# Weights of the last projection in the slab pool, three deep, and a last output tile in three pieces

## The chip, the cores and the metric

The kernel runs on one core of one Trainium2 chip. The metric is the device time of one execution in microseconds, as the median of several runs. A profile is one further execution, recorded by the hardware profiler; its times count from the start of its span. PE is TensorE's matmul unit, PEld its weight loads, DVE is VectorE, ACT is ScalarE, POOL is GpSimd and SP is SyncE, which here issues all DMAs.

## The reference

One step of a two-layer decoder trunk, for 1024 prompt tokens and 8 sample tokens that share the weights (1032 tokens, 1024 features). The first layer joins dilated attention and a state-space scan; the second, where the change lies, is an mLSTM with 8 heads of 256:

```python
def odd_layer(hn, w_in, w_out, ...):
    u = hn @ w_in                                  # 1024 -> q, k, v, o, i, f, z
    ...                                            # convolution, gates
    h, c, n, m = mlstm_chunked(q, k, v, i_t, logf, c0, n0, m0)
    h = sigmoid(o_pre) * h
    h = head_norm(h, norm_w).reshape(b, L, 2048)
    out = (h * silu(z)) @ w_out                    # 2048 -> 1024: the last projection
    return out, ...

hp = hp + mp;  hs = hs + ms                        # residual
y = rmsnorm(h, final_norm_w)                       # over 1024 features, then scaled
```

The sample tokens also update a memory of 8 x 8 x 256 x 256 numbers (`mcs`), which is read and written whole.

## The kernel before, in words

**Arithmetic.** Features lie on partitions, tokens along the free axis. Each float32 operand is split into a high part (ScalarE, line 90: `A.copy(hi, src)`) and a low part (VectorE, line 91: source minus high part), both of type float32r, and a product is three matmuls: high x high, low x high, high x low.

**The last projection** (from line 1588). The weight matrix comes in 32 pieces of 128x1024 (I number them #0 to #31), two for each of eight output rows of 128 features, and this twice: first for tokens 0 to 511 (`hv` 0), then for the other 520 (`hv` 1). `out_f` (line 918) makes one output row: 16 steps over the 2048 inputs, three matmuls in each for each piece of tokens. With `hv` 0 there is one piece of 512, with `hv` 1 there are two, of 264 and 256. Where `done` is not given, the pieces alternate within each step, and each is evicted at the end (VectorE adds the residual, line 935). For the last row alone (`f == 7` of `hv` 1), `done` is given: the pieces run one after the other, and after each comes its part of the closing norm, whose steps are slipped into the next piece's matmuls after its steps 7 and 11 (first the sums over partitions, `stat`, line 188, then the broadcast of the result, line 207), or follow behind the last piece. Then eight scalings (line 221) make the output, with a store for every two.

**Weights.** The class `Weights` loads a piece into a raw buffer (`rawp`, three buffers), and `fetch` splits it into `wh` and `wl`: into two slabs if `slabs` is above zero, which it then counts down, and otherwise into the pool of the input projection's weights, which holds two pairs. `next(ahead)` fetches until more than `ahead` pieces are ready and hands out the first. `wstream` calls it once in eight steps. Two pieces are fetched ahead of the loop (lines 1614 and 1616).

**Buffers.** `S(...)` takes a slab: one of 15 buffers of 128x1040 that the convolutions, the gate, the value weights (`wvh`, `wvl`), the blocks of the sample memory (`dC`), the output rows (`y2`), part of the second half's operands and the final output share. A pool hands out its buffers in the program's order: an instruction that first writes a slab goes after all slabs that were asked for before it in the program, and waits until one is free. The raw pool holds the weights as loaded and, for `hv` 0, also the eight loads `hld` of the projection's operand, each of which is split into `oh` and `ol` (`hT_half`).

**Beside it.** The sample memory's last group runs during `hv` 0: `step(j)` (line 1407) loads block j+1, scales block j on ScalarE, runs eight operations on it on VectorE and stores it; `pump` puts one step after the third row, three after the fourth, three after the fifth and the rest after the sixth.

**Order.** Nothing here sets the order on an engine by hand: the framework's planner runs through the whole program with its own costs, sends each instruction to its engine's queue when its operands and its buffer are there, the earlier in the program first, and so writes one fixed order for each engine and for SP's DMA queue. On the chip each queue then runs strictly in that order.

Of the kernel before, what the change touches and what calls it, by code (L numbers as in the profile page):

```python
# [28 lines left out]
def body(ctx, tc, I, O):  # L29
# [26 lines left out]
    def S(name, dt=F32):  # L56
        return slab.tile([128, 1040], dt, tag="S", name=name)
# [13 lines left out]
    def MM(name="mm"):  # L71
        return ps.tile([128, 512], F32, tag="mm", name=name, bufs=PS_MM)

    def X(name="ax"):
        return ps.tile([128, 512], F32, tag="ax", name=name, bufs=8 - PS_MM)

    def TMP(name="tmp"):
        return tmpp.tile([128, 520], F32, tag="tmp", name=name)

    def D(name, shape):  # L80
        return dr.tile(shape, F32, name=name)
# [33 lines left out]
    class Weights:  # L115
# [8 lines left out]
        def load(self, ahead=1):  # L124
            while len(self.raws) < min(ahead, len(self.srcs)):
                self.raws.append(raw_load(*self.srcs[len(self.raws)]))
# [83 lines left out]
    def hsum(acc, src, first, dve=False):  # L210
        q = acc if first else TMP("sq")[:, : src.shape[-1]]
        if dve:
            V.tensor_tensor(q, src, src, mult)
        else:
            A.activation(q, src, AF.Square)
        if not first:
            V.tensor_tensor(acc, acc, q, add)
# [11 lines left out]
    def pairs(tiles):  # L229
        return lambda k, c0, w: tiles[k // 2][:, (k % 2) * 520 + c0 : (k % 2) * 520 + c0 + w]  # L230
# [88 lines left out]
    def bpump(n):  # L319
        for _ in range(n):  # L320
            if bg:
                bg.popleft()()
# [68 lines left out]
    def pump(n=1):  # L391
        for _ in range(n):
            if side:
                side.popleft()()
# [304 lines left out]
    for f in range(12):  # L699
        w = wq0.next()  # L700
        raw = conv_raw()
        o = S("cout")
# [164 lines left out]
    h1d = D("h1d", [8, 128, T])  # L867
# [47 lines left out]
            r, hi, lo = (t.rearrange("p (j t) -> p j t", j=2)[:, :, :n] for t in (src(p), aop[hv][0][p], aop[hv][1][p]))  # L915
            split(hi, lo, r)

    def out_f(wq, nk, ops, hv, res, dst, done=None):
        n = 520 if hv else 512
        r = TMP("res")  # L920
        load(r[:, :n], res)
        if dst is None:
            dst = r
        pieces = ((0, 264, MM("po")), (264, 256, X("po"))) if hv else ((0, 512, MM("po")),)
        def mms(i, wt, piece):
            c0, m, p = piece
            w, o = wt
            ah, al = (ops[hv][u](i, c0, m) for u in range(2))
            ws = slice(o, o + 128)
            for q, (wt, at) in enumerate(((w[0], ah), (w[0], al), (w[1], ah))):  # L930
                PE.matmul(p[:, :m], wt[:, ws], at, start=i == 0 and q == 0, stop=i == nk - 1 and q == 2)  # L931

        def evac(piece):
            c0, m, p = piece
            V.tensor_tensor(dst[:, c0 : c0 + m], p[:, :m], r[:, c0 : c0 + m], add)

        if done is None:
            for i in range(nk):
                wt = wq(i)
                for piece in pieces:  # L940
                    mms(i, wt, piece)
            for piece in pieces:
                evac(piece)
        else:
            wts = [wq(i) for i in range(nk)]
            steps = deque()
            for piece in pieces:
                for i in range(nk):
                    mms(i, wts[i], piece)
                    if steps and i in ((7, 11) if nk == 16 else (4, 10)):  # L950
                        steps.popleft()()
                evac(piece)
                new = done(dst, piece[0], piece[1])
                steps.extendleft(new[1::-1])
                steps.extend(new[2:])
            while steps:
                steps.popleft()()
        return dst[:, :n]

    def wstream(wts):  # L960
        st_ = {"n": 0}

        def get(i):
            if st_["n"] % 8 == 0:
                st_["w"] = wts.next()
            o = (st_["n"] % 8) * 128
            st_["n"] += 1
            return st_["w"], o

        return get  # L970
# [23 lines left out]
    for f in range(12):  # L994
        w = wq0.next()
# [10 lines left out]
        for c in range(3):  # L1006
            t = TMP("gz")
            c0 = c * CH
            if f >= 8:
                a = TMP("al")  # L1010
                n = min(CH, NP - c0)
# [16 lines left out]
            if c < 2:  # L1028
                o = (f % 2) * 520 + c0
                n = min(CH, 512 - c0)  # L1030
                V.scalar_tensor_tensor(gA[-1][:, o : o + n], t[:, :n], 0.5, a[:, :n], mult, mult)
            if c > 0:
                n = max(512 - c0, 0)
# [6 lines left out]
    def operand(hv, u):  # L1040
        def f(i, c0, w):
            if i < 8:
                return pairs(yop[hv][u])(i, c0, w)
            return pairs(aop[hv][u])(i - 8, c0, w)

        return f
# [47 lines left out]
    ops = [[operand(hv, u) for u in range(2)] for hv in range(2)]  # L1094
    wst = wstream(wqo)
    for hv in range(2):
        n = 520 if hv else 512
        c0 = 512 * hv
        if hv:
            h1 = [S("h1") for _ in range(4)]  # L1100
        for f in range(8):
            dst = pairs(h1)(f, 0, n) if hv else None
# [3 lines left out]
            dst = out_f(wst, 12, ops, hv, I["xT"][:, f, c0 : c0 + n], dst, xn1_tail if hv and f == 7 else None)  # L1106
# [408 lines left out]
    for h in range(8):  # L1515
# [3 lines left out]
        for j in range(4):  # L1519
            t_ = 4 * h + j  # L1520
            if h == 0 and j < 2:
                if j == 0:
                    wts = [wq1.next(1), wq1.next(0)]
# [8 lines left out]
            else:  # L1532
                w = wq1.next()
# [6 lines left out]
            o = S("cout")  # L1540
# [11 lines left out]
        for j in range(2):  # L1552
            w = wq1.next()
# [31 lines left out]
        if h2 == 1:  # L1585
            tail.append(lambda g=g: dml_group(g))

    wqf = Weights([(I["wo1"][f][:, o * 1024 : o * 1024 + 1024], 1024) for _ in range(2) for f in range(8) for o in range(2)])

    hld = deque()  # L1590

    def hT_load(hv, ks):
        for k in ks:
            r = S("hld") if hv else rawp.tile([128, 1040], F32, tag="raw", name="hld")
            rv = r.rearrange("p (j t) -> p j t", j=2)
            load(rv[:, :, :512], hTd[2 * k : 2 * k + 2, :, 512 * hv : 512 * hv + 512].rearrange("j p t -> p j t"))
            hld.append(rv)

    def hT_half(hv, mh, ml, ks):
        n = 520 if hv else 512  # L1600
        for k in ks:
            al = S if hv and k < KB else XS
            mh.append(al("oh", F32R))
            ml.append(al("ol", F32R))
            if not hld:
                hT_load(hv, (k,))
            rv = hld.popleft()
            hi, lo = (t.rearrange("p (j t) -> p j t", j=2) for t in (mh[k], ml[k]))
            if hv:
                G.tensor_scalar(rv[:, :, 512:520], hss[:, 2 * k : 2 * k + 2], 1.0, None, mult)  # L1610
            split(hi[:, :, :n], lo[:, :, :n], rv[:, :, :n])
# [36 lines left out]
    ops = [[pairs(m) for m in mixA], [pairs(m) for m in mixB]]  # L1648
    wst = wstream(wqf)
    for hv in range(2):  # L1650
        n = 520 if hv else 512
        c0 = 512 * hv
        y2 = box[hv] = []
        for f in range(8):
            if f % 2 == 0:
                y2.append(S("y2"))
            dst = pairs(y2)(f, 0, n)
            if hv and f == 7:
                bpump(40)
                out_f(wst, 16, ops, hv, h1d[f][:, c0 : c0 + n], dst, last)  # L1660
                continue
            out_f(wst, 16, ops, hv, h1d[f][:, c0 : c0 + n], dst)
            hsum(yacc[:, hv * 520 : hv * 520 + n], dst, f == 0)
            if hv == 0 and f == 0:
                while tail:
                    tail.popleft()()
                store(O["mn"], nout)
            if hv == 0 and f in (1, 2):
                while dprep and f == 2 or len(dprep) > 2:
                    dprep.popleft()()  # L1670
            if hv == 0:
                pump((0, 0, 1, 3, 3, 2, 0, 0)[f])
            bpump(2)
            if hv == 0 and f == 5:
                hT_load(1, range(3))
            if hv == 0 and f == 6:
                store(O["mms"], dm4)
                store(O["mns"], dn4)
                pump(40)
                hT_half(1, *mixB, range(KB))  # L1680
                hT_load(1, range(3, KB + 4))
            if hv == 0 and f == 7:
                hT_half(1, *mixB, range(KB, KB + 2))
                wqf.fetch()
                hT_load(1, range(KB + 4, 8))
                hT_half(1, *mixB, range(KB + 2, 8))
                wqf.fetch()
        if hv == 0:
            bg.extend(fin_norm(0, 0, 512))
# [174 lines left out]
```

## Time and profile before

| | us |
|---|---|
| runs | 2125.18, 2133.5, 2126.53 |
| median | 2126.53 |
| the profiled execution | 2130.37 |
| its span | 2128.5 |
| TensorE's matmuls busy | 2088.0 (98%) |
| weight loads busy | 1873.7 (88%) |
| VectorE busy | 1348.8 (63%) |
| ScalarE busy | 869.3 (41%) |
| GpSimd busy | 478.0 (22%) |

The profiled execution took 1.9 us more than its span; both are one execution, 3.8 us over the median of the timed runs. Matmuls overlap in the records (one lasts longer than the distance to the next), so the pitch from start to start is what counts. A timeline row gives start, busy time, engine, line and operation, output and inputs, shapes and count, and in brackets the idle time before it with what ended it. Rows of several equal instructions that follow each other are merged (x2 and so on).

### The profile page before, as it was taken

The page shows a single profiled execution, that of the slowest core. Times are in us where ns is not written, and L with a number is a line of the kernel's source. Part 1 is how long each engine was busy: PE and PEld are TensorE (multiplying, and loading weights), DVE is VectorE, ACT ScalarE, POOL GpSimd, SP SyncE. Part 2 cuts the span into 40 slices and gives each one's busy share as a digit, 9 for nine tenths or more (in the row PEclk, how much of TensorE's full clock was granted, in tenths as well). Part 3 has the DMA queues.
Part 4 walks back from the last instruction along what each step waited for, and adds up shares of the span by engine and source line. Part 5 has one row for each costly group of instructions (what it writes and reads, how often), then busy time and mean ns, then how long its engine had stood idle before and what let it go on. Part 6 is the DMA issues. An engine that isn't in the chain of part 4 may idle for free.

```text
span 2128.5 us, 35218 instructions
## 1 busy us (share of the span) xinstructions
PE 2088.0 (98%) x12926; PEld 1873.7 (88%) x12926; DVE 1348.8 (63%) x3208; ACT 869.3 (41%) x1901; POOL 478.0 (22%) x1004
## 2 busy tenths in 40 slices
PE   7999999999999999999999999999999999999998
PEld 6877778998898899989899898898998988987798
DVE  7444478879987657546457565584665755756744
ACT  5434344456644334424335343253342533434321
POOL 4222100114310001241321522314214133141000
PEclk9999999999999999999999999999999999999999
DMA  5222053226575543312114133141331322416742
GB/s 162 73 74 79 14 163 105 85 75 194 185 226 167 169 162 60 90 35 85 50 64 135 41 111 98 40 145 44 99 117 37 116 78 78 140 31 213 268 163 96
DMA packets 162077, 232.30 MB, mean 109 GB/s; under 512 B 41200, under 2 KB 106976, under 8 KB 161904
## 3 DMA queue, kind: packets, MB, share of 16 engines
q1 hardware_dynamic: 161904, 230.04, 34.5%
q8 instruction: 102, 1.67, 0.3%
q14 instruction: 71, 0.58, 0.1%
HBM read 174.35 MB, written 55.62 MB: 108 GB/s over the span
## 4 chain that ended last, share of the span: by engine, by line
PE 85%; DVE 4%; DMA 2%; POOL 2%; ACT 2%; issue 1%; SPq 0%; POOLq 0%; DVEq 0%; ACTq 0%
PE pf L112 36%; PE pvo L112 16%; PE po L931 14%; PE pq L112 4%; PE mN L112 2%; PE mC L112 2%; PE pS L428 2%; PE pO L487 1%; PE mS L1294 1%; PE pT L470 1%; PE py L771 1%; POOL mCl L91 1%; PE mH L1355 1%; PE psl L777 1%; PE mS L1296 1%
## 5 line engine op out<-in xcount | busy, mean ns | idle before, releaser
L112 PE MATMUL pf<-yh,wh 128*128 128x344 f32 x1152 | 370.2, 321 | 0.0
L112 PE MATMUL pf<-yl,wh 128*128 128x344 f32 x1152 | 368.9, 320 | 0.0
L112 PE MATMUL pf<-yh,wl 128*128 128x344 f32 x1152 | 368.5, 320 | 0.0
L91 DVE TENSOR_TENSOR wl<-raw,wh 128x1024 fp32r<-128x1024 f32 x128 | 159.0, 1242 | 146.1 <-ACT wh L90 145.3
L90 ACT CAST wh<-raw 128x1024 fp32r<-128x1024 f32 x128 | 134.2, 1049 | 256.9 <-PE po L931 99.6
L112 PEld LDWEIGHTS pf<-yh,wh 128*128 128x128 f32 x1152 | 216.9, 188 | 1.3 <-ACT craw L242 1.0
L112 PEld LDWEIGHTS pf<-yl,wh 128*128 128x128 f32 x1152 | 216.5, 188 | 0.0
L112 PEld LDWEIGHTS pf<-yh,wl 128*128 128x128 f32 x1152 | 216.4, 188 | 0.0
L112 PE MATMUL pvo<-wvh,yh 128*128 128x512 f32 x512 | 206.3, 403 | 0.0
L112 PE MATMUL pvo<-wvh,yl 128*128 128x512 f32 x512 | 202.0, 394 | 0.0
L112 PE MATMUL pvo<-wvl,yh 128*128 128x512 f32 x512 | 201.5, 394 | 0.0
L112 PE MATMUL pf<-xh,wh 128*128 128x344 f32 x576 | 191.6, 333 | 0.0
L112 PE MATMUL pf<-xl,wh 128*128 128x344 f32 x576 | 186.8, 324 | 0.0
L112 PE MATMUL pf<-xh,wl 128*128 128x344 f32 x576 | 186.7, 324 | 0.0
L1282 DVE TENSOR_SCALAR mx<-mx,mbs,md 128x256 f32<-128x256 f32 x64 | 26.4, 413 | 177.7 <-POOL md L1281 177.7
L250 DVE SCALAR_TENSOR_TENSOR cout<-craw,mcw,cout 128x1024 f32<-128x1024 f32 x96 | 123.3, 1285 | 14.0 <-ACT cout L248 11.9
L931 PE MATMUL po<-oh,wl 128*128 128x512 f32 (+2 forms) x384 | 123.4, 322 | 2.8 <-DVE wl L91 2.7
L931 PE MATMUL po<-oh,wh 128*128 128x512 f32 (+2 forms) x384 | 123.6, 323 | 1.2 <-ACT oh L90 1.2
L931 PE MATMUL po<-ol,wh 128*128 128x512 f32 (+2 forms) x384 | 123.7, 323 | 0.0
L112 PEld LDWEIGHTS pvo<-wvh,yl 128*128 128x128 f32 x512 | 96.2, 188 | 22.6
L112 PEld LDWEIGHTS pvo<-wvh,yh 128*128 128x128 f32 x512 | 96.3, 188 | 20.6 <-issue 1.3
L112 PEld LDWEIGHTS pvo<-wvl,yh 128*128 128x128 f32 x512 | 96.3, 188 | 20.0
(440 smaller groups left out, 4995.7 us busy)
## 6 DMA issues: line engine op xcount, KB each, us to landing
raw<-in_wo SPq DMA_DIRECT2D x56, 512.0 KB
raw<-in_wq SPq DMA_DIRECT2D x32, 512.0 KB
raw<-in_wvo SPq DMA_DIRECT2D x32, 512.0 KB
dC<-in_mcs SPq DMA_DIRECT2D x32, 512.0 KB
out_mcs<-dC SPq DMA_DIRECT2D x32, 512.0 KB
raw<-in_wf SPq DMA_DIRECT2D x24, 512.0 KB
sE<-acd SPq DMA_DIRECT2D x16, 512.0 KB
raw<-in_wz SPq DMA_DIRECT2D x16, 512.0 KB
```

Of the source, the lines that this page charges most:

```text
L90: A.copy(hi, src)
L91: eng.tensor_tensor(lo, src, hi.bitcast(F32), sub)
L112: PE.matmul(out, l, r, start=i == 0, stop=i == n - 1)
L250: V.scalar_tensor_tensor(o[:, :NP], raw[:, j : j + NP], w4[:, j : j + 1], o[:, :NP], mult, add)
L428: PE.matmul(p[:, :n], qT[g][hs, qs], kT[g][hs, ks], start=True, stop=True)
L470: PE.transpose(pt[:, h * n + k : h * n + k + 128], P[:, k : k + 128], ident)
L487: PE.matmul(po[h * 64 : h * 64 + 64, qs], v, PT[:, h * n + k * 128 : h * n + k * 128 + 128], start=j + k == 0, stop=j == 7 and k == nk - 1)
L771: PE.matmul(o, xd[:, h], Ev[:, h], start=True, stop=True)
L777: PE.matmul(pl, bt, xx[:, 512:1024], start=True, stop=True)
L931: PE.matmul(p[:, :m], wt[:, ws], at, start=i == 0 and q == 0, stop=i == nk - 1 and q == 2)
L1282: V.tensor_scalar(x, x, bs[:, 6:7], d[:, 2:3], sub, mult)
L1294: PE.matmul(pS[:, 0:128], hd["k"][j][:, tok], hd["q"][j][:, tok], start=j == 0, stop=j == 1)
```

## The change

Three edits. The last projection's `Weights` gets `slabs=9`: pieces #0 to #8 are split into slabs, the others into the two pairs as before. `wstream` asks `next` for two pieces ahead in place of one as long as slabs are left to be taken; the first layer's projection, which has none, keeps one. And `out_f` takes the token pieces as an argument: the last row is cut into 264, 128 and 128 tokens, the other rows of `hv` 1 stay at 264 and 256.

```diff
-    def out_f(wq, nk, ops, hv, res, dst, done=None):
+    def out_f(wq, nk, ops, hv, res, dst, done=None, cuts=(264, 256)):
...
-        pieces = ((0, 264, MM("po")), (264, 256, X("po"))) if hv else ((0, 512, MM("po")),)
+        pieces = [(sum(cuts[:i]), m, (X if i else MM)("po")) for i, m in enumerate(cuts)] if hv else ((0, 512, MM("po")),)
...
         def get(i):
             if st_["n"] % 8 == 0:
-                st_["w"] = wts.next()
+                st_["w"] = wts.next(2 if wts.slabs else 1)
...
-    wqf = Weights([(I["wo1"][f][:, o * 1024 : o * 1024 + 1024], 1024) for _ in range(2) for f in range(8) for o in range(2)])
+    wqf = Weights([(I["wo1"][f][:, o * 1024 : o * 1024 + 1024], 1024) for _ in range(2) for f in range(8) for o in range(2)], slabs=9)
...
             if hv and f == 7:
                 bpump(40)
-                out_f(wst, 16, ops, hv, h1d[f][:, c0 : c0 + n], dst, last)
+                out_f(wst, 16, ops, hv, h1d[f][:, c0 : c0 + n], dst, last, (264, 128, 128))
```

## Rows read from the trace of the kernel before

**Rows 1.** Waits of PE from 1880 us: waiter, releaser, total us, times, longest.

```profile
PE po L931 <- DVE wl L91: 2.7, 1, 2.7
PE po L931 <- ACT oh L90: 1.2, 1, 1.2
```

**Rows 2.** Timeline of PE (start, us): projection's first matmul; around the stall.

```profile
1923.35 0.48 PE L931 MATMUL po<-oh,wh 128*128 128x512 f32 x1
...
1993.32 0.39 PE L931 MATMUL po<-oh,wh 128*128 128x512 f32 x1
1993.55 0.39 PE L931 MATMUL po<-ol,wh 128*128 128x512 f32 x1
1996.68 0.51 PE L931 MATMUL po<-oh,wl 128*128 128x512 f32 x1 [2.74 <-DVE wl L91]
```

**Rows 3.** The chain that ended last (start, us, what), three steps.

```profile
1927.87 4.49 DMA hld<-hTd
...
1981.44 6.81 DMA dC<-in_mcs
...
1996.68 7.83 PE po L931 x26
```

**Rows 4.** Windows: us, busy us by engine, clock granted, DMA share, GB/s.

```profile
1990.00:2000.00 10.00, 7.26 (x28) 5.51 (x27) 10.00 (x23) 4.14 (x5) 0.00 (x0) 0.89 0.76 256
...
2080.00:2100.00 20.00, 20.00 (x169) 20.00 (x168) 8.57 (x12) 5.28 (x6) 0.00 (x0) 1.00 0.37 124
```

**Rows 5.** Timeline of VectorE: weight splits, an eviction, sample block, late split.

```profile
1960.63 1.23 DVE L91 TENSOR_TENSOR wl<-raw,wh 128x1024 fp32r<-128x1024 f32 x1 [0.16 <-ACT wh L90]
...
1977.37 1.23 DVE L91 TENSOR_TENSOR wl<-raw,wh 128x1024 fp32r<-128x1024 f32 x1
...
1982.39 0.69 DVE L935 TENSOR_TENSOR y<-po,res 128x512 f32<-128x512 f32 x1 [0.49 <-PE po L931]
...
1989.46 0.88 DVE L1417 SCALAR_TENSOR_TENSOR dC<-dvb,dkw,dC 128x256 f32<-128x256 f32 x2 [4.35 <-ACT dC L1413]
...
1995.41 1.22 DVE L91 TENSOR_TENSOR wl<-raw,wh 128x1024 fp32r<-128x1024 f32 x1
```

**Rows 6.** Timeline of SP's DMA issues before the late block.

```profile
1981.00 0.34 SPq L1422 DMA_DIRECT2D out_mcs<-dC  x1
1981.44 1.85 SPq L1364 DMA_DIRECT2D dC<-in_mcs  x3
```

**Rows 7.** Timeline of ScalarE: cast of weight #0; of the last block's values.

```profile
1843.96 1.05 ACT L90 CAST wh<-raw 128x1024 fp32r<-128x1024 f32 x1 [1.08 <-DMA raw<-in_wo]
...
1914.06 0.37 ACT L90 CAST mvh<-pvo 128x256 fp32r<-128x256 f32 x1 [2.57 <-PE pvo L112]
```

**Rows 8.** Timeline of PE: last tile's first piece, then its second piece.

```profile
2103.66 0.28 PE L931 MATMUL po<-oh,wh 128*128 128x264 f32 x1
...
2109.53 0.28 PE L931 MATMUL po<-oh,wh 128*128 128x256 f32 x1
...
2112.24 0.28 PE L931 MATMUL po<-oh,wl 128*128 128x256 f32 x1
```

**Rows 9.** Timeline of PEld: sums over partitions, 128 columns and 8 columns.

```profile
2112.24 0.31 PEld L188 LDWEIGHTS pst<-ones,yacc 128*128 128x128 f32 x2
...
2112.92 0.30 PEld L188 LDWEIGHTS pst<-ones,sq 128*128 128x128 f32 x2
2113.24 0.10 PEld L188 LDWEIGHTS pst<-ones,yacc 128*8 128x8 f32 x2
```

**Rows 10.** Timeline of the end: last eviction, last broadcast, last scalings.

```profile
2117.70 0.42 DVE L935 TENSOR_TENSOR y<-po,res 128x256 f32<-128x256 f32 x1 [0.21 <-PE po L931]
...
2120.87 1.22 PE L207 MATMUL prb<-dg,ones 128*128 128x128 f32 x4 [1.41 <-DVE dg L206]
...
2122.13 3.22 DVE L221 SCALAR_TENSOR_TENSOR fin<-y,fnw,prb 128x256 f32<-128x256 f32 x8 [0.32 <-PE prb L207]
```

**Rows 11.** Timeline of VectorE: two operations of 128 columns from PSUM.

```profile
1934.60 0.60 DVE L1358 SCALAR_TENSOR_TENSOR mhT<-mH,mnw,msz 128x128 f32<-128x128 f32 x2
```
## The prediction

> **What bounds the kernel now.** I read the page first: PE is busy for 98% of the span, and no engine beside TensorE for more than 63%, so only time in which PE stands still, or in which the program goes on after PE's last matmul, can be won. Then the waits of PE in the last 250 us [rows 1], where the changed code runs: there are few, and the longest is 2.7 us, in line 931 (the last projection), on `wl`, the low half of a weight. The timeline of PE shows the place [rows 2]: matmuls follow each other every 0.23 us, but the one after 1993.55 starts at 1996.68. By the chain [rows 3] the 26 matmuls from there on take 7.83 us; at 0.23 they would take 5.98. The windows say why [rows 4]: PE's granted clock is 0.89 as a mean of those ten microseconds, so behind the stall it ran for a while at the lower of its two levels, 1.2 GHz. The stall therefore costs 2.74 + 1.85 = 4.6 us.
>
> Its cause is on VectorE's queue [rows 5]. VectorE waits 4.35 us for `dC` (a block of the sample memory), runs fifteen operations on two such blocks, and only then, in order, makes `wl` at 1995.41. The block is late because its load was issued at 1981.44 [rows 6] and took 6.81 us [rows 3]; on SP's queue it stands behind the store of the block before it, which waits for VectorE. The missing weight is the thirteenth (I call it #12, counting from #0): it goes into the one of two buffers that #10 leaves, so it can't be split much sooner.
>
> The other place is the end. The last eviction starts at 2117.70, and the last scaling ends at 2122.13 + 3.22 = 2125.35 [rows 10]: 7.65 us in which PE does next to nothing.
>
> **The slab weights and the stall.** No instruction is added: the nine splits run as before (1.05 us on ScalarE [rows 7], 1.23 on VectorE [rows 5]), into other buffers and at other times. Weights #0 to #8 no longer alternate between two buffers, and #9 and #10 find both of these empty, since the input projection's weights are done. So all up to #10 can be split well before PE needs them, as fast as the three raw buffers feed them. From #11 on nothing changes: #11 waits for #9's buffer, #12 for #10's. What changes for #12 is the crowd on VectorE: in the kernel before, four weight splits sit among the sample blocks from 1960.63 to 1977.37 [rows 5]; done earlier, they let the fourth block finish up to 4.9 us sooner, its store with it, and the load behind the store [rows 6]. Data that are there at about 1988 now (1981.44 + 6.81) come near 1984, and fifteen operations of 5.95/15 = 0.4 us, behind one of 1.2 on ScalarE, end near 1991, before PE runs dry at 1993.8. I take the stall as gone: -4.6. The other end is 0: slab buffers are handed out in program order, and these loads come behind the tile `y2` of the fifth output row, first written at 1982.39 [rows 5], next to which they issue now; if that holds them, nothing is won.
>
> **The same slabs at the start.** This is what the edit costs. Of 15 slabs the last head holds 4 (q, k), 2 (gate) and 8 (value weights), and a sample block has the last. In the kernel before, #0 is split at 1843.96 [rows 7] and #1 soon after, in spare time. Now they need slabs, and the first come free when the last block's attention products have read q and k, just behind the cast of its values at 1914.06 [rows 7]. Until then their raw copies hold two of the three raw buffers, and the eight operand loads `hld` of the projection go through the same three: all but the first now come behind the first weight split, near 1917. The projection starts at 1923.35 [rows 2], so #0 is in time. VectorE gets two splits more between 1915 and 1925 (2.5 us), but loses operand splits there, which come later. One operand takes 4.49 us of load [rows 3] and 1.05 + 1.23 of splitting, so three buffers turn out one per 2.26 us. Each gives PE six matmuls of the first output row and six of the second, 12 x 0.23 = 2.8 us of work, if the order written by the planner takes both: PE is then fed. The ends: -1.3 (today's wait on `oh`, 1.2 [rows 1], goes) and +5.3 (PE takes the first row alone, 1.4 us per operand, and waits 0.88 us for each of six). The nearest row is today's wait, so a value near nothing; for loads longer than the planner thinks I put +0.5.
>
> **The tail.** The last output row's second piece, 256 tokens, becomes two of 128: 96 matmuls in place of 48. A matmul of 264 takes (2109.53 - 2103.66)/48 = 0.122 us, one of 256 (2112.24 - 2109.53)/23 = 0.118 [rows 8]. The trace has no 128-token matmul of this type. Bounds: 0.059 if only the tokens count, 0.118 if nothing gets shorter. The nearest rows are the sums over partitions, which load a 128x128 array for one column: a load and its matmul take (2112.92 - 2112.24)/6 = 0.113, while two loads of 8 columns last 0.10 together against 0.31 [rows 9]. So filling the array sets a floor, and each of our matmuls fills it anew. I take 0.113: 96 x 0.113 - 48 x 0.118 = +5.2. The first new piece also sends its sums (0.45) and broadcast (0.25) through the second's matmuls: +0.7.
>
> Off the end comes, for 128 columns in place of 256: eviction and square, each 0.42 to about 0.28 (two such operations take 0.60 [rows 11]), -0.3; one block of sums for two, -0.45; one diagonal, -0.2; half of the broadcast's 1.22 us [rows 10], -0.6; eight scalings at 0.28 for 0.40, -0.95; a smaller last store, -0.3. Together -2.8. The scalings of the earlier pieces run on VectorE beside the matmuls. Sum +3.1; with the bounds of the matmul, -2.1 to +3.6.
>
> The Trainium skill speaks to this price (TensorE: Matmul & The Clock Gate, section Back-to-back issue gap): for a stream of load and matmul pairs it gives about 81 ns each at 128 columns. By that figure the tail would be 96 x 0.081 - 5.66 + 0.7 - 2.8 = 0.0, an estimate from that page. No row here shows such a stream, and the 0.113 of the sums is slower; the sum goes by the row.
>
> **Sum.** -4.6 + 0.5 + 3.1 = -1.0 us. The profiled execution took 2130.37 us (span 2128.5); by it the changed kernel would take 2129.4. The timed runs have their median at 2126.53, 3.8 lower, so I predict 2125.5.
>
> **The rivals.**
> - *The stall stays.* For it: the two buffers from #11 on and the coupling to `y2` are as before. Against it: the splits between 1960 and 1979 go. Then +0.5 + 3.1: 2130.1. That the change doesn't do what it says (slabs granted so late that "three deep" never exists) ends in the same place and is counted here.
> - *Slower: the start starves PE.* #0 and #1 in the raw buffers push seven operand loads behind 1917, and in PE's strict order each missing operand stops the projection. It decides from the point where the planner puts the first row's matmuls one behind the other, trusting in loads shorter than 4.49 us: +5.3, and +1.85 more if PE falls to 1.2 GHz as it did at 1996. With the stall gone and the tail: -4.6 + 7.1 + 3.1 = +5.6, 2132.1; with the stall, 2136.7. For it: PE waits on this pool already [rows 1]. Against it: the second row can fill in.
> - *Narrow matmuls are cheap*: the array's load hides better than in the sums, and one takes 0.06 to 0.08. For it: the sums are in plain float32, the projection in another type. Against it: PEld is busy without a gap at 256 tokens [rows 4]. The tail is then -2.1 to 0, the whole -6.2 to -4.1: 2121.4.
>
> **How the numbers follow.** Forecast 0.45, its own range 2121 to 2130; the stall stays 0.20; starved start 0.18; cheap matmuls 0.14; something else 0.03. The range takes in the cheap matmuls and the starved start without the stall, and some scatter: 2118.5 to 2134.5. A measurement of this kernel tells about 0.5%, 10.6 us, from no change. All parts at their best win 4.6 + 1.3 + 2.1 = 8.0, so "faster" by over 0.5% needs something that I haven't seen: 0.04. "Slower" needs a start worse than its bound, with the stall and the tail on top: 0.07. "Same": 0.89.
>
> **What would show it.** No PE wait on `wl` near 1990 us, and PE's clock at 1.0 there: the stall step. The first output weight cast near 1915, and PE's waits between 1923 and 1940 under 2 us in all: the start. A pitch of `po` matmuls at 128 tokens near 0.113, and under 5.5 us from the last eviction to the last scaling's end: the tail. It is wrong if that pitch is near 0.06, if PE waits over 4 us near the start, or if a wait on a weight turns up elsewhere.

## The result, and the profile after

The changed kernel took 2140.02 us (median, 2138.55 to 2142.58) against 2127.8 (2125.18 to 2133.5) for the kernel before: a ratio of 1.0058, 95% interval 1.0047 to 1.0069, 12 us slower. The forecast was 2125.5, the range 2118.5 to 2134.5. The profiled execution took 2138.93, its span is 2137.2, against 2130.37 and 2128.5 before. More than the whole difference between these two lies in the last 30 us. It is not one execution's: the mean granted clock was 0.991 to 0.994 in each of the six executions of the changed kernel, and 0.995 to 0.999 in those of the kernel before.

The timeline of PE, the last output tile of the changed kernel (start, us); it answers to [rows 8, 9]:

```profile
2101.54 0.28 PE L931 MATMUL po<-oh,wh 128*128 128x264 f32 x1
...
2107.41 0.22 PE L931 MATMUL po<-oh,wh 128*128 128x128 f32 x1
...
2109.92 0.28 PE L931 MATMUL po<-oh,wl 128*128 128x128 f32 x1
2110.04 0.33 PE L188 MATMUL pst<-ones,yacc 128*128 128x1 f32 x2
...
2114.30 0.41 PE L931 MATMUL po<-oh,wl 128*128 128x128 f32 x1
...
2121.34 0.41 PE L931 MATMUL po<-oh,wl 128*128 128x128 f32 x1
```

The first 24 matmuls of 128 tokens start every (2109.92 - 2107.41)/23 = 0.109 us. From 2114.30 on, 33 steps take 7.04 us, 0.213 each. The windows of the same stretch (columns as in [rows 4]) say why:

```profile
2110.00:2112.00 2.00, 2.00 (x22) 1.96 (x21) 0.21 (x2) 0.00 (x0) 0.51 (x1) 1.00 0.00 0
2112.00:2114.00 2.00, 1.90 (x14) 1.69 (x12) 0.70 (x3) 0.00 (x0) 0.74 (x2) 0.84 0.00 0
2114.00:2116.00 2.00, 2.00 (x10) 1.98 (x10) 1.87 (x5) 0.00 (x0) 0.00 (x0) 0.50 0.01 4
...
2126.00:2128.00 2.00, 2.00 (x12) 2.00 (x11) 1.89 (x8) 0.00 (x0) 0.00 (x0) 0.50 0.32 92
```

Read the first number behind the last bracket, 1.00, 0.84, 0.50: within the narrow matmuls PE's granted clock falls from 2.4 to 1.2 GHz and does not come back. PE's records cover 1.90 of 2.00 us where it falls, and all of each window from 2114 to 2128. (The records overlap, so a window that they cover does not tell how much of the array worked.) In the kernel before they leave up to 0.22 us of a window open, and the clock is 1.00 up to 2120, behind the tile's last matmul:

```profile
2116.00:2118.00 2.00, 1.78 (x15) 1.67 (x14) 1.59 (x4) 0.00 (x0) 0.00 (x0) 1.00 0.00 0
```

The end on VectorE, to be laid beside [rows 10] (last eviction, last scalings):

```profile
2128.19 0.29 DVE L935 TENSOR_TENSOR y<-po,res 128x128 f32<-128x128 f32 x1 [0.30 <-PE po L931]
...
2131.69 2.16 DVE L221 SCALAR_TENSOR_TENSOR fin<-y,fnw,prb 128x128 f32<-128x128 f32 x8 [0.95 <-PE prb L207]
```

From the last eviction to the last scaling it is 2131.69 + 2.16 - 2128.19 = 5.66 us, 2.0 less than before. So a shorter end is there, though not quite the one forecast (under 5.5).

PE's waits from 1840 us (columns as in [rows 1]): the one long wait on `wl` is gone, two short ones have come.

```profile
PE po L931 <- DVE wl L91: 1.4, 2, 1.0
...
PE po L931 <- ACT oh L90: 0.6, 2, 0.4
```

The two lie in the start, and the longer one is

```profile
1927.69 0.50 PE L931 MATMUL po<-oh,wl 128*128 128x512 f32 x1 [0.99 <-DVE wl L91]
```

Behind 14 matmuls of the projection PE wants the low half of #2, which VectorE has just made. A wait on a weight elsewhere was one of the prediction's signs of being wrong.

Three landmarks of PE before the last tile, first of the kernel before, then of the changed one: the last block of the previous stage (`mS`), the first sample product within the projection (`pvb`), and the product just behind the place of the stall (`pdr`).

```profile
1913.86 0.61 PE L1294 MATMUL mS<-cout 128*128 128x128 f32 x4
...
1947.72 0.70 PE L1388 MATMUL pvb<-v,blkT 16*128 16x259 f32 x2
...
2004.44 0.61 PE L1426 MATMUL pdr<-dnum,blk 128*16 128x258 f32 x2
```
```profile
1914.11 0.61 PE L1294 MATMUL mS<-cout 128*128 128x128 f32 x4
...
1950.60 0.70 PE L1388 MATMUL pvb<-v,blkT 16*128 16x259 f32 x2
...
2002.49 0.61 PE L1426 MATMUL pdr<-dnum,blk 128*16 128x258 f32 x2
```

With them the difference splits into parts that add up, in these two executions (between the landmarks PE runs the same number of matmuls in both). Up to `mS`: +0.25. From `mS` to `pvb`, the start: 36.49 for 33.86, +2.6. From `pvb` to `pdr`, the stall: 51.89 for 56.72, -4.8. The rest up to the last tile's second piece: -0.2. From there to the last scaling's end: 2107.41 to 2133.85 is 26.44 us, before 2109.53 to 2125.35 was 15.82: **+10.6**. Together +8.5, of a span that is 8.7 longer. (The profiled execution of before was 2.6 us above its median, that of after 1.1 below its own, which makes the rest of the 12.2.)

### The profile page after: what moved, and what is told of

The parts are those of the page before. It is cut to its first block, busy times and chain, and to the rows that moved or that the text cites. A ratio compares the mean times of both kernels' runs of the same rounds, so it can differ in the third digit from the quotient of the medians.

```text
span 2137.2 us, 35337 instructions
## 1 busy us (share of the span) xinstructions
PE 2100.2 (98%) x12974; PEld 1885.9 (88%) x12974; DVE 1352.7 (63%) x3218; ACT 868.6 (41%) x1902; POOL 480.0 (22%) x1005
## 4 chain that ended last, share of the span: by engine, by line
PE 84%; DVE 3%; DMA 2%; ACT 2%; POOL 2%; issue 1%; SPq 0%; POOLq 0%; DVEq 0%; ACTq 0%
PE pf L112 36%; PE pvo L112 16%; PE po L931 15%; PE pq L112 4%; PE mN L112 2%; PE mC L112 2%; PE pS L428 2%; PE pO L487 1%; PE mS L1294 1%; PE pT L470 1%; PE mH L1355 1%; PE py L771 1%; PE mS L1296 1%; DMA mE<-mud 1%; DMA hld<-hTd 1%
## 5 line engine op out<-in xcount | busy, mean ns | idle before, releaser
L931 PE MATMUL po<-oh,wl 128*128 128x512 f32 (+3 forms) x400 | 130.0, 325 | 1.4 <-DVE wl L91 1.4
L931 PE MATMUL po<-oh,wh 128*128 128x512 f32 (+3 forms) x400 | 130.3, 326 | 0.6 <-ACT oh L90 0.6
L931 PE MATMUL po<-ol,wh 128*128 128x512 f32 (+3 forms) x400 | 130.1, 326 | 0.1
```

## The experiments

Two questions stood: what brings the clock down in the tail, and whether the slabs did what the prediction said. The kernels are told in the order of the questions. Below, "tail" is the time from the first matmul of the last tile to the end of the last scaling: before 2103.66 to 2125.35, 21.69 us; after 2101.54 to 2133.85, 32.31.

**Slabs alone.**

```diff
-                out_f(wst, 16, ops, hv, h1d[f][:, c0 : c0 + n], dst, last, (264, 128, 128))
+                out_f(wst, 16, ops, hv, h1d[f][:, c0 : c0 + n], dst, last)
```

> The slabs as in the changed kernel, the last tile in 264 and 256 tokens as before. Theory A (the loss is in the tail, where the 128-token matmuls bring the granted clock down): 10.6 us of tail go, the stall's gain (4.8) and the start's loss (2.6) stay, so a span near 2126.5 and a clock of 1.0 in the last 20 us; timed 1 to 3 us under the kernel before. Rival B (the clock falls at the end because of what the slabs do ahead of it): the clock is 0.5 there with 256-token matmuls too, and the span stays above 2132.

Measured: 2127.49 us for 2128.97, ratio 0.9994 (0.9985 to 1.0003); the span profiled is 2128.5. The windows (columns as in [rows 4]) show the clock at 1.0 through the tail, and something that was not expected: the stall is back.

```profile
1990.00:2000.00 10.00, 7.97 (x30) 6.05 (x29) 10.00 (x24) 4.50 (x5) 0.00 (x0) 0.86 0.74 246
...
2116.00:2118.00 2.00, 1.70 (x14) 1.60 (x13) 1.67 (x5) 0.00 (x0) 0.00 (x0) 1.00 0.02 7
```

So the loss is in the tail, not a late effect of the slabs (rival B falls). And up to the last tile this kernel has the same order of instructions on every engine as the changed one, yet PE stood still for 2.0 us near 1995: the stall is not gone, it comes in some executions and not in others. What goes with it is the load of the late block of the sample memory, here by the chain that ended last (as in [rows 3]), and in the changed kernel by ScalarE's first operation on the block, whose load was issued at 1982.70:

```profile
1981.77 6.55 DMA dC<-in_mcs
```
```profile
1987.36 1.15 ACT L1413 ACTIVATE dC<-dC,dss 128x1024 f32<-128x1024 f32 x1 [0.97 <-DMA dC<-in_mcs]
```

From the issue to that operation it took 6.6 us here and 4.7 in the changed kernel. Of the six executions profiled with this order, the four without the stall have 4.7 to 4.8 us there, the two with it 5.9 and 6.6. Why the load takes longer in some is not shown.

**Cuts alone.**

```diff
-    wqf = Weights([...], slabs=9)
+    wqf = Weights([...])
```

> No slabs; the last tile in 264, 128 and 128 tokens. Theory A: the projection up to the last tile as in the kernel before, with the wait of 2.7 us on a weight; then PE's clock falls to 0.5 within the 128-token matmuls, pitch 0.21, tail about 10.6 us longer: span near 2139, timed some 11 us over the kernel before. Rival B (only together with the slabs does the clock fall): pitch 0.11 to the end, tail +3.1, span near 2131.6.

Measured: 2138.78 us, ratio 1.005 (1.0035 to 1.0065). The cuts alone bring the loss. Here the clock falls sooner, right behind the first piece's sums (PE's 12 one-column matmuls at 2107.53 to 2108.6), while PE's records cover all of the window:

```profile
2106.00:2108.00 2.00, 2.00 (x21) 2.00 (x19) 0.00 (x0) 0.04 (x1) 0.00 (x0) 1.00 0.04 8
2108.00:2110.00 2.00, 2.00 (x16) 1.96 (x15) 0.49 (x4) 0.00 (x0) 1.02 (x2) 0.66 0.00 0
2110.00:2112.00 2.00, 2.00 (x11) 2.00 (x10) 0.20 (x2) 0.00 (x0) 0.23 (x1) 0.50 0.00 0
```

**The same matmuls over 256 columns.** Theory A: narrow matmuls bring the clock down; rival C: the sums and broadcasts between them do.

```diff
-            c0, m, p = piece
+            c0, m, p = piece if piece[1] != 128 else (264, 256, piece[2])
...
-            V.tensor_tensor(dst[:, c0 : c0 + m], p[:, :m], r[:, c0 : c0 + m], add)
+            V.tensor_tensor(dst[:, c0 : c0 + m], p[:, c0 - 264 : c0 - 264 + m] if m == 128 else p[:, :m], r[:, c0 : c0 + m], add)
```

> As the changed kernel, but the 96 matmuls of the two 128-token pieces each run over all 256 tokens of the old piece; each piece still evicts only its own 128. Twice the columns, the same instructions, sums and broadcasts between them. Theory A (narrow matmuls bring the clock down): the clock stays 1.0, the pitch is 0.118, and the tail is some 7 us shorter than in the changed kernel although PE computes more: span near 2130. Rival C (the sums and broadcasts that break into the stream, now three times, bring the clock down): it falls at the same place, pitch 0.22 to 0.24, span 2137 to 2139.

Measured: 2132.59 us, ratio 1.0017 (1.0007 to 1.0026): 7.4 us less than the changed kernel, with 96 x 128 = 12,288 columns more to compute. The clock holds (its mean is 0.997 to 0.999 in all ten executions):

```profile
2114.00:2116.00 2.00, 1.96 (x16) 1.74 (x15) 1.00 (x4) 0.00 (x0) 0.12 (x1) 1.00 0.00 0
...
2120.00:2122.00 2.00, 2.00 (x18) 2.00 (x18) 0.63 (x3) 0.00 (x0) 0.55 (x1) 1.00 0.41 142
```

The tail is 25.7 us, 4.0 over before. That is what three pieces cost when the clock stays.

**The narrow matmuls without a break.**

```diff
-                    if steps and i in ((7, 11) if nk == 16 else (4, 10)):
-                        steps.popleft()()
```

> As the changed kernel, but nothing breaks into the 96 narrow matmuls: the sums, broadcasts and scalings of all three pieces come behind the last matmul. Theory A: the clock falls to 0.5 within the 96 matmuls all the same; from the first 128-token matmul to the last takes 13 us or more. Rival C (the breaks bring it down): it stays 1.0 through all of them, 96 x 0.111 = 10.7 us. The end gets longer by some 6 us in either case, since the scalings of the first two pieces no longer lie beside matmuls.

Measured: 2141.2 us, ratio 1.0058 (1.0043 to 1.0073), the time lost in the longer end: 18.2 us from PE's last matmul of the projection for 5.7 in the changed kernel, twice the 6 us more that were expected. (The edit also moves these steps behind the last row of the first layer's projection, near 795 us, far from the windows read here.) But the clock, in windows of the 96 narrow matmuls:

```profile
2108.00:2110.00 2.00, 2.00 (x20) 2.00 (x20) 0.34 (x1) 0.43 (x1) 0.00 (x0) 1.00 0.04 8
...
2116.00:2118.00 2.00, 2.00 (x20) 2.00 (x20) 0.00 (x0) 0.00 (x0) 0.00 (x0) 1.00 0.00 0
```

It stays 1.00 to the last. Theory A as I had put it falls: narrow matmuls alone did not bring the clock down; nor did these breaks alone, by the run before. It fell where both came together (theory E).

**Narrow matmuls with one break.**

```diff
-                    if steps and i in ((7, 11) if nk == 16 else (4, 10)):
+                    if steps and (i == 7 and len(steps) == 10 if len(pieces) == 3 else i in ((7, 11) if nk == 16 else (4, 10))):
```

> As the changed kernel, but of all sums and broadcasts only the sums of the first piece (12 matmuls of one column, 1.1 us) break into the 96 narrow matmuls, after the 24th; the others come at the end. Theory E (narrow matmuls and a break together bring the clock down, and one break is enough): the clock falls to 0.5 soon behind the sums, the later matmuls at 0.21. Rival F (it takes the broadcasts too, or several breaks): 1.0 through all 96, pitch 0.111.

Measured, in one run: 2147.24 us. One block of 12 sums among the narrow matmuls is enough:

```profile
2110.00:2112.00 2.00, 2.00 (x23) 1.99 (x21) 0.00 (x0) 0.00 (x0) 0.00 (x0) 1.00 0.03 8
2112.00:2114.00 2.00, 2.00 (x18) 1.97 (x17) 0.21 (x2) 0.00 (x0) 1.21 (x2) 0.79 0.00 0
2114.00:2116.00 2.00, 2.00 (x11) 2.00 (x11) 0.00 (x0) 0.00 (x0) 0.00 (x0) 0.50 0.00 0
...
2124.00:2126.00 2.00, 2.00 (x11) 2.00 (x11) 0.00 (x0) 0.00 (x0) 0.00 (x0) 0.50 0.00 0
```

The last lines show more: 72 narrow matmuls follow from 2112.09 on without any break; the clock falls near their beginning and stays at 0.50. In the run before, an unbroken stream of them left it up; here, at the lower level, it did not bring it back.

**Wide matmuls with a long break.**

```diff
-            for i, acc in enumerate(accs):
+            for i, acc in [*enumerate(accs)] * (3 if n == 264 and type(post) is int else 1):
```

> The kernel before, the last tile in 264 and 256 tokens, but the sums of its first piece are run three times over (36 matmuls of one column in place of 12, some 3.3 us in place of 1.1). Theory E: a break three times as long brings the clock down between matmuls of 256 columns too; then the 24 matmuls behind it take 0.21 to 0.24 each, +2.2 for the sums and +2.5 for the clock. Rival G (256-token matmuls keep the clock up whatever breaks in): 1.0 to the end, only +2.2.

Measured, in one run: 2130.43 us. The clock falls among 256-token matmuls too, and here it returns:

```profile
2112.00:2114.00 2.00, 2.00 (x24) 1.97 (x21) 0.69 (x4) 0.00 (x0) 1.25 (x2) 0.86 0.00 0
2114.00:2116.00 2.00, 2.00 (x10) 1.75 (x9) 0.49 (x2) 0.00 (x0) 0.00 (x0) 0.50 0.00 0
2116.00:2118.00 2.00, 1.84 (x13) 1.76 (x12) 1.25 (x4) 0.00 (x0) 0.00 (x0) 0.79 0.21 76
```

So 256 tokens are not safe in themselves (rival G falls): with 12 sums between them the clock held, with 36 it fell. The tail is 25.0 us, 3.3 over before, for the 4.7 expected.

**The narrow pieces first.**

```diff
-                out_f(wst, 16, ops, hv, h1d[f][:, c0 : c0 + n], dst, last, (264, 128, 128))
+                out_f(wst, 16, ops, hv, h1d[f][:, c0 : c0 + n], dst, last, (128, 128, 264))
```

> As the changed kernel, but the last tile in the order 128, 128 and 264 tokens. Only four sums (0.4 us) and two broadcasts break into the second narrow piece; the sums of that one break into the wide piece. Theory E (the clock falls where narrow matmuls and a break come together; a short break may not do): either 1.0 to the end, then 96 x 0.111 + 48 x 0.122 = 16.5 us for 11.5, +5, and the wide piece's end as before, span near 2133; or it falls in the second narrow piece and comes back within the wide one, span near 2136. Rival H (128-column matmuls in number, wherever they stand, bring the clock down for the rest of the kernel): 0.5 to the end, span over 2140.

Measured: 2134.16 us (2130.91 to 2138.03), ratio 1.0023 (1.0013 to 1.0033). Same pieces, same matmuls; but only 4 sums and 2 broadcasts stand among narrow ones. In the profiled execution, the fastest of the ten, the clock holds:

```profile
2106.00:2108.00 2.00, 2.00 (x20) 2.00 (x20) 0.16 (x1) 0.00 (x0) 0.39 (x1) 1.00 0.03 8
2108.00:2110.00 2.00, 2.00 (x20) 2.00 (x19) 1.16 (x5) 0.00 (x0) 0.16 (x1) 1.00 0.00 0
```

Its tail is 2098.80 to 2125.52, 26.7 us, 5.0 over before: again the price of three pieces at the upper clock. Rival H falls. Of its ten executions the four with a mean clock of 0.998 took 2130.9 to 2133.2, the six at 0.995 to 0.997 took 2134.1 to 2138.0. Perhaps the clock falls for a while in those; no trace shows it.

**The sums spread.**

```diff
-                    if steps and i in ((7, 11) if nk == 16 else (4, 10)):
+                    if steps and i in ((3, 5, 7, 11) if piece[1] == 128 and piece[0] == 264 else (7, 11) if nk == 16 else (4, 10)):
...
-        return [stat, rest, bcast] + [lambda k=k: one(k) for k in range(8)]
+        return ([lambda j=j: stat(j) for j in range(3)] if n == 264 else [stat]) + [rest, bcast] + [lambda k=k: one(k) for k in range(8)]
```

> The changed kernel, with one change: the 12 sums of the first piece (1.1 us of one-column matmuls in one block between the narrow matmuls) stand in three blocks of four, behind the 12th, 18th and 24th narrow matmul. Nothing else moves, not the broadcasts either. If it is the length of one break among narrow matmuls that brings the clock down: it stays 1.0 to PE's last matmul, pitch 0.111, and the tail is some 7 us shorter than in the changed kernel, span near 2130 to 2132. If it is the sum of narrow matmuls and breaks however they are spread: the clock falls near the broadcasts as before, span 2137 or more.

Measured: 2140.05 us, ratio 1.0059 (1.0042 to 1.0076). The timeline of PE shows the fall even sooner, before the third block of sums:

```profile
2107.23 0.36 PE L188 MATMUL pst<-ones,sq 128*128 128x1 f32 x2
...
2108.34 0.36 PE L188 MATMUL pst<-ones,sq 128*128 128x1 f32 x2
...
2109.04 0.28 PE L931 MATMUL po<-ol,wh 128*128 128x128 f32 x1
2109.16 0.38 PE L931 MATMUL po<-oh,wl 128*128 128x128 f32 x1
2109.47 0.20 PE L188 MATMUL pst<-ones,yacc 128*8 128x1 f32 x2
```

It is not the length of one break: spreading the same sums did not help. Eight sums stood among the narrow matmuls when the clock fell, four in the run before, whose traced execution kept it. Whether their number is what matters, no run shows.

**Late slabs.** Now the slabs: #0 and #1 stay in the two ordinary buffers, #2 to #8 go into slabs.

```diff
-                if self.slabs:
+                if self.slabs and len(self.srcs) < self.below:
...
-    wqf = Weights([...], slabs=9)
+    wqf = Weights([...], slabs=7, below=30)
...
-                out_f(wst, 16, ops, hv, h1d[f][:, c0 : c0 + n], dst, last, (264, 128, 128))
+                out_f(wst, 16, ops, hv, h1d[f][:, c0 : c0 + n], dst, last)
```

> Weights #0 and #1 in the ordinary two buffers as in the kernel before, #2 to #8 in slabs; the last tile in 264 and 256 tokens. What the prediction said of the stall (splits done early relieve VectorE, the late block comes sooner): the start's loss of 2.6 us goes, the stall stays away, span near 2123.7. Theory D (the slabs relieve nothing: the late weight is made at 1994 to 1996 as before, and the changed kernel only did not wait for it because PE came 2.9 us later): PE is back at its old times in the first rows, and waits 1 to 3 us for the low half of #12 again, with or without 1.9 us of lower clock behind it: span 2126.5 to 2128.5.

Measured: 2125.4 us for 2126.97, ratio 0.9992 (0.9983 to 1.0001); the span profiled is 2124.6. The late weight (VectorE), its block's load (SP), and windows around the old stall:

```profile
1991.92 1.22 DVE L91 TENSOR_TENSOR wl<-raw,wh 128x1024 fp32r<-128x1024 f32 x1
```
```profile
1979.95 1.76 SPq L1364 DMA_DIRECT2D dC<-in_mcs  x3
```
```profile
1990.00:2000.00 10.00, 10.00 (x45) 8.11 (x44) 9.02 (x19) 2.52 (x4) 0.00 (x0) 1.00 0.86 299
```

In the changed kernel the same two stood at

```profile
1994.49 1.23 DVE L91 TENSOR_TENSOR wl<-raw,wh 128x1024 fp32r<-128x1024 f32 x1
```
```profile
1982.70 1.81 SPq L1364 DMA_DIRECT2D dC<-in_mcs  x3
```

Counted from `mS` (1915.31 with late slabs), the load is issued 64.6 us on and the weight split at 76.6; before [rows 5, 6] it was 67.6 and 81.5, in the changed kernel 68.6 and 80.4. So the prediction's mechanism (splits done early bring the block forward) is there with the start left as it was: 3.0 us for the load and 4.9 for the weight, of which the other 1.9 come from a load that landed within 4.75 us (issue to ScalarE's first operation) for 6.8 before. The nine slabs from the start push the load back by 1.0 and bring the weight forward by 1.2. Theory D describes the changed kernel, not the late slabs. The times between the landmarks over the executions that were profiled with one of three orders (the kernel without a break and the one with the weight on GpSimd have orders of their own):

| order up to the last tile | `mS` to `pvb`, us | `pvb` to `pdr`, us | sum of means |
|---|---|---|---|
| before (before, cuts alone, long break) | 33.9, 33.4, 33.5 | 56.7, 54.4, 54.1 | 88.7 |
| slabs from the start (after, slabs alone, 256 columns, narrow first, spread, one break) | 36.5, 35.8, 36.1, 36.2, 35.9, 36.0 | 51.9, 55.7, 53.4, 51.9, 51.9, 51.9 | 88.9 |
| late slabs (late, 328 + 192, 392 + 128) | 33.8, 33.6, 33.5 | 51.8, 51.8, 51.8 | 85.5 |

Between `pvb` and `pdr` 51.8 to 51.9 is PE without a stall. The nine slabs give back at the start what they win at the stall; late slabs win 3.2 us of PE's time. The timed 1.6 us are not told apart from nothing.

**The late weight on GpSimd.** The kernel before, with only #12's low half moved.

```diff
+    wqf = Weights([...], first=(V,) * 12 + (G,))
```

> The kernel before, with one change: the low half of weight #12 is made by GpSimd, not by VectorE. Theory D (the wait is VectorE's queue, where the split stands behind the sample blocks): the cast ends at 1990.4, GpSimd takes some 2.6 us (twice its 1.34 for 516 columns), the weight is there near 1993.0, PE comes at 1993.8 and does not wait: 2.7 + 1.85 us less, span near 2124. Rival: the next weight, still on VectorE behind the blocks, is late in its place, and less than 2 us are won.

Measured: 2131.45 us, ratio 1.0018 (1.0009 to 1.0027), slower. GpSimd had the weight ready at 1991.27 + 2.56 = 1993.83 and PE did not wait for it. The next one was late instead, and longer (PE's timeline, then windows):

```profile
2004.03 0.80 PE L931 MATMUL po<-oh,wl 128*128 128x512 f32 x1 [2.97 <-DVE wl L91]
```
```profile
2000.00:2010.00 10.00, 7.03 (x18) 4.37 (x17) 7.37 (x20) 1.57 (x2) 2.08 (x4) 0.69 0.89 308
```

VectorE ran the sample blocks on and came to #13 only at 2002.76. The rival holds: taking one split out of the crowded queue moved the wait to the next.

**Two cuts other than 264 and 256**, on the late slabs: `(328, 192)` and `(392, 128)` in place of `(264, 256)`.

> As the run with late slabs (#0 and #1 in the ordinary buffers, #2 to #8 in slabs), but the last tile in 328 and 192 tokens. If the clock holds behind the first piece's sums: 48 x (0.147 + 0.111) = 12.4 us of matmuls for 11.5, +0.9, against 1.2 less in evictions, broadcast and scalings at the end: -0.3, span near 2124.5. If 192 columns fall to 0.5 behind the sums as 128 did: 24 matmuls at 0.21 in place of 0.11, +2.5, broadcasts and end slower too, span near 2128. Up to the last tile the instructions are those of the run with late slabs, so its row times show over again whether the late weight is in time (theory D with late slabs: no PE wait on it).

> As the run with late slabs, the last tile in 392 and 128 tokens: one narrow piece, with the sums of the wide one (16 matmuls, 1.4 us) after its 24th matmul. Theory E: the clock falls behind these sums as in the changed kernel; 48 x (0.175 + 0.111) = 13.7 us, +2.2, 24 at the lower clock +2.5, the end 2.4 shorter but partly at the lower clock: span 2126 to 2128. Rival (it takes the 96 narrow matmuls): the clock holds, span near 2124.5.

Measured: 2128.49 us for 2129.93, ratio 0.9994 (0.9986 to 1.0002), and 2129.51, ratio 0.9996 (0.9987 to 1.0005). Windows, first with 192 tokens, then with 128:

```profile
2112.00:2114.00 2.00, 1.98 (x18) 1.83 (x17) 0.70 (x4) 0.00 (x0) 1.26 (x2) 1.00 0.00 0
2114.00:2116.00 2.00, 1.90 (x18) 1.72 (x16) 1.44 (x4) 0.00 (x0) 0.00 (x0) 1.00 0.00 0
```
```profile
2112.00:2114.00 2.00, 2.00 (x14) 2.00 (x14) 0.57 (x4) 0.00 (x0) 1.41 (x2) 0.70 0.00 0
2114.00:2116.00 2.00, 2.00 (x10) 1.72 (x8) 0.56 (x3) 0.00 (x0) 0.00 (x0) 0.50 0.00 0
```

At 192 tokens the clock held with the same 12 sums; in a single narrow piece of 128 with 16 sums it fell. Neither cut pays: the tails are 24.5 and 25.2 us for 21.7. With 192 the span came out at 2128.4, 4 over my 2124.5: the last eviction starts 2.3 us after PE's last matmul, because VectorE still scales the wide first piece. No version beats the kernel before by more than the interval; late slabs with the old cut come nearest.

## Why the prediction was wrong

**The failed step is the tail's matmul term.** "I take 0.113: 96 x 0.113 - 48 x 0.118 = +5.2." The pitch at the upper clock was right: 0.109 to 0.111 us, so +5.0. But only the first 37 of the 96 ran at it. The other 59 took 0.213, which adds 59 x 0.102 = +6.0. The breaks, for which I had +0.7, came to +1.6 as the remainder, partly at the lower clock. The end gave 2.0 for my 2.8 (from the first sum behind PE's last matmul: 7.85 before, 5.90 after). 5.0 + 6.0 + 1.6 - 2.0 = +10.6 for +3.1; the upper bound of +3.6 assumed that nothing could make a narrow matmul dearer than a wide one. The price without the fall is shown by the 256 columns (+4.0) and by the narrow pieces first (+5.0): even then the cut loses.

I had the clock in [rows 4] and in a rival, but as a matter of waits only: PE stands still, and the clock falls behind it. That a stream in which PE's records leave no gap can lose it was in none of my cases. The Trainium skill (TensorE: Matmul & The Clock Gate, section HAM oscillation — how this bites in real kernels) names PE's idle time in waits as what brings the clock down. By that it would have stayed up here; the traces do not agree, for in the window of the fall the records cover 2.00 of 2.00 us in the cuts alone (0.66 granted) and with one break (0.79). The Trainium skill (TensorE: Matmul & The Clock Gate, section Back-to-back issue gap) also gives 81 ns per pair at 128 columns, by which the tail would have been 0.0. Measured are 109 to 111 ns: the nearest row was the better guide.

**The stall** met its price in the execution profiled (-4.8 for -4.6), and that was luck. The block's load was to come sooner; in the changed kernel it came later, and the weight only 1.2 us sooner. At its old pace PE would have run dry at 1993.8 + 0.25 and waited 1.7 us for a weight that was ready at 1994.49 + 1.23 = 1995.7. It did not wait because the start had made it late, and because the load landed in 4.7 us: of the six executions profiled with this order, the two with slower loads had the stall again (1.5 and 3.9 us, over 51.9 without). With late slabs the mechanism is there. But that the weight came 4.9 us sooner, the very number of "they let the fourth block finish up to 4.9 us sooner", is chance: 3.0 are the earlier load, the rest is the load's own time.

The price itself was that of one slow execution. The two others profiled with the order of before take 54.4 and 54.1 us between `pvb` and `pdr` for its 56.7, so the stall cost them 2.5 and 2.2. My sum took off 4.6 for the stall, and then 3.8 because that execution was slow; some 2.5 of this (an estimate from the three executions) are the same time.

**The start** cost +2.6 for my +0.5 (+2.5 as a mean of six against three), within its ends of -1.3 and +5.3. The cause was named: #0 and #1 hold raw buffers until a slab comes free. Leaving just these two in the ordinary buffers takes all of it away (33.6 for 33.6). I weighted it by today's wait, as the nearest row; but that wait was there with all operands on time, and the change made seven of them later, by 4.9 to 12.3 us. Yet in the execution profiled PE waited longer for the low halves of #2 and #3 (1.4 us) than for operands (0.6): the planner turned to the second row sooner, and VectorE's queue was late for it.

**The range** held no case of both the tail at its measured price and the rest; with +10.6 in place of +3.1 the sum would have been 2133.0, and with the start 2135.1. Of the 4.9 us that are left to 2140.0, 1.3 lie in the kernel before, whose median came out at 2127.8 when it was run beside the changed one, for 2126.53; some 2.5 are the stall's time that was taken off twice; the rest is not traced. "Slower" had 0.07, with a start beyond its bound as the only way to it.

## What to carry to other kernels

Before a matmul is made narrower, count what else runs on PE in that stretch: one-column sums and small broadcasts among 128-token matmuls halved the clock here for the rest of the kernel, though PE's records left next to no gap, while either alone did not in the executions traced. Price such a cut at both clock levels, and look at the granted clock of the stretch before reading anything else. When a buffer is added to feed a late stage earlier, see that it does not move what the start of the stage needs; and when one operation is taken out of a crowded queue, price the next one in it. A stall that hangs on a load's time should be priced from several executions, not from one.

## What the runs showed of the hardware that was not expected

- PE's granted clock went from 1.0 to 0.5 with PE's records covering 1.90 to 2.00 of 2.00 us in the window of the fall: among 128-token matmuls with 8 to 16 sums of one column between them (five kernels), and among 256-token matmuls with 36. It held with 96 narrow matmuls unbroken, with 4 sums among narrow ones, and with 12 among 192-token and 256-token ones. One execution of each was traced.
- The two directions differ: 96 unbroken narrow matmuls left the clock up where it was up, 72 left it at 0.50 where it was down; 256-token ones with the clock down had it back (0.50, 0.79, 1.00 in windows of 2 us).
- With the same order of instructions, one load of 512 KB took 4.7 to 6.6 us from its issue to its first use, and the stall came and went with it.
- Computing twice the columns, same instructions, was 7.4 us faster (2132.59 for 2140.02).
- What exactly the chip weighs stays open; the runs show which mixtures fell and which held, not a rule.
